# Head tiles of 64 in three transformer blocks: columns by fours, rotation over full rows, halves stacked by DMA

## The chip, the core and the metric

The kernel runs on one core of one Trainium2 chip. The metric is the device time of one execution in microseconds (us); the median of three runs counts.

## The reference

Three different transformer blocks run one after the other over 512 tokens of 1024 channels, in float32. Each has feed-forward parts (2816 wide, gated) and a mixer. The change touches the attention in the mixers of block 1 and of the two layers of block 3. Cut to that:

```python
# block 1: 8 heads of 64, causal, with a forget term
logits = q @ k.T * 64**-0.5 + cum[q] - cum[k]
out = softmax(where(kpos <= qpos, logits, NEG_INF)) @ v
# block 3, two layers: kinds A (8 heads, keys chosen by an index) and B (4 pairs of heads)
q, k = apply_rope(q), apply_rope(k)      # x1*c - x2*s, x2*c + x1*s; x1, x2 the halves of 64
out_a = softmax(where(selected, q @ k.T * scale, -inf)) @ v
out_b = (softmax(q0 @ k0.T) - lam * softmax(q1 @ k1.T)) @ v
```

## The kernel before, in words

Activations lie with channels on the 128 partitions and tokens in the columns. The 512 tokens are two halves of 256 (`hf`), and every phase is written for both halves, the second lagging by some 20 to 30 us (`LAGS`), so that both use a weight while it is in the ring. A product in about float32 accuracy is three fp16 products of high and low halves (`three`, `gemm`): one output tile of 128 x 256 from 1024 channels is 24 matmuls. Weights come in slots of 512 KB on SP's queue into 3 staging buffers (L360), ACT casts the high half (L362), DVE the low half (L363) into a ring of 12.

Nothing fixes the order of the work by hand: a list scheduler orders each engine's instructions at build time by a priority, and a buffer that isn't free holds an instruction back. The priority is a virtual time, advanced with `adv` (2.6 us for one projection), and `boost(us)` moves a group ahead by so many us: rotations have RB = 80, the splitting into heads PB = 10 in block 3 and MB = 80 in block 1.

Keys and queries come out of 8 projection tiles per set: 4 tiles of keys, 4 of queries, each two heads of 64 rows. There are ten such sets: block 1 for each half, and in block 3 two layers, kinds A and B, two halves. In block 3 `rotated` (a function in `mixer3`) takes a tile from PSUM: ACT copies four times 32 rows so that the halves change places (L1286, tile `rsw`), DVE multiplies the tile by the cosine (L1287) and the swapped one by the sine (L1288) and adds them (L1289). It is also used for the three tiles of the index heads (32 wide).

The class `Heads` holds the result. A score is two matmuls over 128 rows: a key tile has its fp16 high half in 64 rows and its low half in the other 64; a query tile has the high half in both places, and a second query tile (`low`) has the low half in 64 rows and zeros, set by a memset on POOL, in the rest. `put` fills them for each head of the tile: ACT writes the high half (L676, in block 1 L679 with the scale), DVE the low half (L677, L680), and for queries ACT copies the high half into the other 64 rows (L682). `scores` issues the two matmuls per 256 keys. PSUM has two buffers per half for projections (`pmm`); a half has 7 temporary buffers of 1 KB per partition (`t1k`).

After a set of heads come the value projections, two `token_gemm` of 24 matmuls with 512 columns, and then attention: scores, row maximum (L641), exponential (L646), reciprocal (L648), transposes and the product with the values. Beside kind B's heads the index scores are computed, and DVE takes the 16 rounds of eight maxima (L1342, L1343).

Of the kernel before, what the change touches and what calls it, by code (L numbers as in the profile page):

```python
# [11 lines left out]
F16 = mybir.dt.float16  # L12
# [7 lines left out]
TH = 256  # L20
# [55 lines left out]

def pack_tm(w):
    return np.ascontiguousarray(w.reshape(4, 2, 128, 512).transpose(0, 2, 1, 3)).reshape(4, 128, 1024)


def small_cols(w):
# [75 lines left out]
def prepare(inp):  # L157
# [12 lines left out]
        a[f"gu1{n}"] = pack_pair(f("ffn_w_gate")[0, n], f("ffn_w_up")[0, n])  # L170
        a[f"dn1{n}"] = pack_cm(f("ffn_w_down")[0, n])
    w = f("w_in")[0]
    a["m1_qk"] = pack_cm(w[:, 1024:2048])
    a["m1_v"] = pack_tm(w[:, 2048:2560])
    a["m1_f"] = small_cols(w[:, 2560:2568])
    a["m1_u"] = pack_cm(w[:, 0:512])
# [34 lines left out]
    for l in range(2):  # L211
        a[f"gu3{l}"] = pack_pair(f("w_gate_3")[l], f("w_up_3")[l])
        a[f"dn3{l}"] = pack_cm(f("w_down_3")[l])
        w = f("w_in_3")[l]
        iq = w[:, 1536:1792].reshape(D, 4, 2, 2, 16).transpose(0, 1, 3, 2, 4).reshape(D, 256)
        ik = w[:, 1792:1824].reshape(D, 2, 16)
        ike = np.zeros((D, 2, 2, 2, 16), w.dtype)
        for e in range(2):
            ike[:, e, :, e, :] = ik
        a[f"m3_i{l}"] = pack_cm(np.concatenate([iq, ike.reshape(D, 128)], 1))  # L220
        a[f"m3_w{l}"] = small_cols(w[:, 1824:1832])
        a[f"m3_a{l}"] = pack_cm(np.concatenate([w[:, 512:1024], w[:, 0:512]], 1))
        a[f"m3_va{l}"] = pack_tm(w[:, 1024:1536])
        a[f"m3_b{l}"] = pack_cm(np.concatenate([w[:, 2344:2856], w[:, 1832:2344]], 1))
        a[f"m3_vb{l}"] = pack_tm(w[:, 2856:3368])
        a[f"m3_o{l}"] = pack_cm(f("w_out_3")[l])
    a["cols"] = np.ascontiguousarray(np.concatenate(cols.parts, 1))
# [5 lines left out]
    a["consts"] = np.ascontiguousarray(np.concatenate(list(c.values()), 1))  # L233
    a["foxsel"] = fox_selector()
    a["headrows"] = head_rows()
    a["rope64"] = rope_rows(32)
    a["rope32"] = rope_rows(16)
    return a, cols.at, at

# [4 lines left out]
def tile_three_blocks(ctx: ExitStack, tc: tile.TileContext, d, col_at, con_at, out, phases=None):  # L244
# [13 lines left out]
    kvp = pool("kvp", 9)  # L258
    prp = pool("prp", 3)
    tin = pool("tin", 2)  # L260
    psm = pool("psm", 2, space=bass.MemoryType.PSUM)
    pss = pool("pss", 2, space=bass.MemoryType.PSUM)

# [394 lines left out]
    class Heads:  # L658
# [1 line left out]


        def __init__(self, alloc, hf, query):
            self.t = [alloc(hf, [128, 2, 2, TH], F16, "hd") for _ in range(2)]
            self.low = [alloc(hf, [128, 4, TH], F16, "hl") for _ in range(2)] if query else None
            if query:
                for e in range(2):
                    G.memset(self.low[e][64 - 64 * e:128 - 64 * e], 0.0)

        def put(self, j, src, scale=None):
            t = self.t[j // 2][:, j % 2]  # L670
            for e in range(2):
                a, b = slice(64 * e, 64 * e + 64), slice(64 - 64 * e, 128 - 64 * e)
                hi = t[a, e]
                lo = t[b, e] if self.low is None else self.low[e][a, j]
                if scale is None:
                    S.activation(hi, src[a], AF.Copy)  # L676
                    V.tensor_tensor(lo, src[a], hi, op=OP.subtract)  # L677
                else:
                    S.activation(hi, src[a], AF.Copy, scale=scale)  # L679
                    V.scalar_tensor_tensor(lo, src[a], scale, hi, op0=OP.mult, op1=OP.subtract)  # L680
                if self.low is not None:
                    S.activation(t[b, e], hi, AF.Copy)  # L682

    def scores(s, q, ks, j, e, c, nk):
        for kh, c0, n in keys(nk):
            k = ks[kh].t[j // 2][:, j % 2, e]
            mm(s[:, c0:c0 + n], q.t[j // 2][:, j % 2, e, c], k[:, :n], start=c0 == 0, stop=False)
            mm(s[:, c0:c0 + n], q.low[e][:, j, c], k[:, :n], start=False, stop=False)

    def keys(nk):  # L690
        return [(0, 0, min(nk, TH))] + ([(1, TH, nk - TH)] if nk > TH else [])
# [16 lines left out]
    def mixer1(hf):  # L708
# [21 lines left out]
            m1["carry"] = 0.0  # L730

        kt, qt_ = Heads(kv2k, hf, False), Heads(m2k, hf, True)
        for j in range(8):
            adv(hf, 2.6)
            p = pmm(hf, [128, TH], name="pp")
            gemm(p, W("m1_qk"), (j + 4) % 8 * KD, KD, px)
            with boost(MB):
                (kt if j < 4 else qt_).put(j % 4, p, 1.0 / WS if j < 4 else 0.125 / WS)
        m1["k", hf] = kt

        adv(hf, 2.6)
# [34 lines left out]
        with boost(BOOST["m1a"]):  # L776
            for qt in range(2):
                nk = (2 * hf + qt + 1) * 128
                yb = m2k(hf, name="yb")
                ybs.append(yb)  # L780
                for h in range(8):
                    j = h // 2
                    s = psmall(hf, [128, 512], name="ps")
                    scores(s, qt_, [m1["k", i] for i in range(hf + 1)], j, h % 2, slice(qt * 128, (qt + 1) * 128), nk)
# [468 lines left out]
    def mixer3(hf, l):  # L1253
# [65 lines left out]
        with later(SELB):  # L1319
            for qt in range(2):  # L1320
# [26 lines left out]
        def logits(qs, ks, j, e, qt, nk, bar):  # L1347
            s = psmall(hf, [128, 512], name="ps")
            scores(s, qs, [m3[ks, i] for i in range(hf + 1)], j, e, slice(qt * 128, (qt + 1) * 128), nk)
# [6 lines left out]
        ybs, yas = [], []  # L1356

        kb, qb = Heads(kv2k, hf, False), Heads(m2k, hf, True)
        for j in range(8):
            dst = t1k(hf, name="rot")  # L1360
            rotated(f"m3_b{l}", j, dst, "rope64", 1.0 / WS if j < 4 else 0.125 / WS)
            with boost(PB):
                (kb if j < 4 else qb).put(j % 4, dst)
        m3["kb", hf] = kb
        vb = []
        for tt in range(2):
# [6 lines left out]
        with boost(BOOST["m3b"]):  # L1373
            for qt in range(2):
                nk = (2 * hf + qt + 1) * 128
                nb = nk // 128

                yb = m2k(hf, name="yb")
                ss = tiny(hf, 4, "dss")
                for h in range(4):  # L1380
                    s = logits(qb, "kb", h, 0, qt, nk, None)
                    p0, r0, s0 = softmax(hf, s, nk)
                    p1, r1, _ = softmax(hf, logits(qb, "kb", h, 1, qt, nk, None), nk)
# [17 lines left out]
        for j in range(8):  # L1401
            dst = t1k(hf, name="rot")
            rotated(f"m3_a{l}", j, dst, "rope64", 1.0 / WS if j < 4 else 0.125 / WS)
            with boost(PB):
                (ka if j < 4 else qa).put(j % 4, dst)
        m3["ka", hf] = ka
        va = []
        for tt in range(2):
# [6 lines left out]
        with boost(BOOST["m3a"]):  # L1415
            for qt in range(2):
# [2 lines left out]

                ya = m2k(hf, name="ya")  # L1420
                for h in range(8):
                    s = logits(qa, "ka", h // 2, h % 2, qt, nk, bars.get(qt))
# [102 lines left out]
```

## Time and profile before

| what | value |
|---|---|
| median of 3 runs | 3486.3 us (3482.32 to 3499.97) |
| the profiled execution | 3491.3 us, its span 3489.5 us |
| PE, DVE, ACT busy | 95%, 62%, 44% of the span |
| mean granted clock of TensorE | 0.98 |
| block 1's mixer, block 3's two mixers, by the trace | about 390 to 620, 2100 to 2450, 2780 to 3100 us |

A row of groups reads: line, engine, operation, tile written <- tiles read, shape, count | busy us in all, mean ns of one | idle time of the engine before them and what ended it. Waits are "who waited <- for what". PE's matmuls are pipelined, so a busy PE isn't PE at its peak.

### The profile page before, as it was taken

Reading aid. Unit: us, or ns where it says so; the run is one execution under the profiler, and the core shown is the slowest. Engines: PE = TensorE matmul, PEld = TensorE weight load, DVE = VectorE, ACT = ScalarE, POOL = GpSimd, SP = SyncE. Lnnn points to the kernel's source line nnn. Section 1 sums busy time; section 2 is a strip of 40 time slices with the busy share of each in tenths; the row PEclk is TensorE's granted clock in tenths of the full one; section 3 lists DMA queues with packets and bytes.
Section 4 is the critical chain, followed back from the end, with each engine's and each line's share of the span. In section 5 each row is a group of like instructions: output and inputs, shape, how many; then the busy total and the mean of one; then the engine's idle time right before and its main releaser. Section 6 shows DMA issues by size and latency. Waiting matters only on the chain.

```text
span 3489.5 us, 71768 instructions
## 1 busy us (share of the span) xinstructions
PE 3315.7 (95%) x30120; PEld 2801.9 (80%) x30120; DVE 2154.7 (62%) x5164; ACT 1542.0 (44%) x3337; POOL 19.1 (1%) x24
## 2 busy tenths in 40 slices
PE   8999999999999999998789999889999998999998
PEld 5888767888888888886578887667888876688887
DVE  8953758744374437677984438896544488855433
ACT  4232465433243324424243336886333278843331
POOL 0000000000000000000000000000000000000000
PEclk9999999999999999987899999999999999999999
DMA  8832313233323222201022222112232321123331
GB/s 309 308 110 91 107 55 131 73 103 101 101 91 103 97 98 97 65 5 34 19 85 98 97 100 97 55 43 67 92 103 97 105 86 53 51 68 109 104 98 48
DMA packets 103283, 327.85 MB, mean 94 GB/s; under 512 B 12328, under 2 KB 17832, under 8 KB 102704
## 3 DMA queue, kind: packets, MB, share of 16 engines
q1 hardware_dynamic: 102960, 323.28, 27.8%
q8 instruction: 235, 3.85, 0.4%
q14 instruction: 88, 0.72, 0.1%
HBM read 321.14 MB, written 2.10 MB: 93 GB/s over the span
## 4 chain that ended last, share of the span: by engine, by line
PE 74%; DVE 12%; ACT 10%; issue 2%; DMA 1%; SPq 0%; ACTq 0%; DVEq 0%
PE pgu L314 37%; PE po L314 19%; PE pp L314 4%; PE ps L314 3%; ACT rsw L1286 3%; DVE wr L363 2%; ACT wr L362 2%; DVE mix L963 1%; PE pt L314 1%; PE pT L314 1%; ACT hd L676 1%; PE pxy L314 1%; ACT prob L646 1%; PE pw L314 1%; PE ps L653 1%
## 5 line engine op out<-in xcount | busy, mean ns | idle before, releaser
L314 PEld LDWEIGHTS <-wr 128*128 128x128 f16 x24000 | 2346.8, 98 | 329.9 <-issue 27.6
L314 PE MATMUL pgu<-hh,wr 128*128 128x256 f16 x12672 | 1401.9, 273 | 8.0 <-DVE fac L525 2.3
L363 DVE SCALAR_TENSOR_TENSOR wr<-st,wr 128x1024 f16<-128x1024 f32 x524 | 640.3, 1223 | 348.4 <-ACT wr L362 339.7
L314 PE MATMUL po<-act,wr 128*128 128x256 f16 x6336 | 700.3, 273 | 0.1
L362 ACT ACTIVATE wr<-st 128x1024 f16<-128x1024 f32 x524 | 551.1, 1053 | 316.2 <-PE pgu L314 127.4
L314 PE MATMUL pp<-hh,wr 128*128 128x256 f16 x3072 | 379.3, 274 | 4.3 <-DVE rot L1287 2.1
L522 ACT ACTIVATE fth<-pgu 128x256 f32<-128x256 f32 x264 | 101.0, 383 | 580.7 <-PE pgu L314 580.5
L523 DVE SCALAR_TENSOR_TENSOR fth<-fth,pgu 128x256 f32<-128x256 f32 x264 | 110.9, 420 | 353.2 <-ACT fth L522 353.1
L314 PE MATMUL po<-mix,wr 128*128 128x256 f16 x1536 | 197.3, 281 | 17.6 <-DVE wr L363 9.8
L443 ACT ACTIVATE act<-fac 128x256 f16<-128x256 f32 x264 | 109.9, 416 | 183.0 <-DVE fac L525 182.7
L314 PE MATMUL pt<-wr,hh 128*128 128x512 f16 x576 | 143.9, 380 | 0.7 <-DVE wr L363 0.6
L444 DVE TENSOR_TENSOR act<-fac,act 128x256 f16<-128x256 f32 x264 | 111.3, 422 | 49.2 <-ACT act L443 48.8
L491 DVE TENSOR_TENSOR acc<-acc,sq 128x256 f32<-128x256 f32 x84 | 35.4, 421 | 149.9 <-ACT sq L490 149.9
L1286 ACT ACTIVATE rsw<-pp 32x256 f32<-32x256 f32 x304 | 114.1, 375 | 19.9 <-PE pp L314 15.6
L525 DVE SCALAR_TENSOR_TENSOR fac<-fth,pgu 128x256 f32<-128x256 f32 x264 | 110.7, 419 | 7.7
L431 ACT ACTIVATE sq<-x 128x256 f32<-128x256 f32 x154 | 56.0, 409 | 134.2 <-DVE x L500 129.6
L484 ACT ACTIVATE y<-po 128x256 f32<-128x256 f32 x64 | 24.4, 382 | 204.6 <-PE po L314 204.6
L963 DVE SCALAR_TENSOR_TENSOR mix<-glu,cols,mix 128x256 f32<-128x256 f32 x240 | 101.9, 475 | 0.1
L314 PEld LDWEIGHTS <-hh 128*128 128x128 f16 x768 | 62.2, 99 | 47.3 <-issue 1.6
L641 DVE TENSOR_REDUCE amx<-ps 128x1 f32<-128x128 f32 (+3 forms) x160 | 77.1, 486 | 34.5 <-PE ps L314 32.9
L500 DVE SCALAR_TENSOR_TENSOR x<-po,x 128x256 f32<-128x256 f32 x64 | 27.0, 422 | 108.9 <-PE po L314 108.8
L646 ACT ACTIVATE prob<-ps,amx 128x128 f32<-128x128 f32 (+3 forms) x160 | 84.0, 525 | 18.9 <-DVE amx L641 17.4
(357 smaller groups left out, 2926.4 us busy)
## 6 DMA issues: line engine op xcount, KB each, us to landing
st<-in_gu_dram SPq DMA_DIRECT2D x264, 512.0 KB, 3.5
st<-in_dn_dram SPq DMA_DIRECT2D x132, 512.0 KB, 3.5
adw<-in_w_ada_dram SPq DMA_DIRECT2D x112, 256.0 KB, 5.5
st<-in_m_o_dram SPq DMA_DIRECT2D x32, 512.0 KB, 3.5
adr<-in_w_ada_dram SPq DMA_DIRECT2D x16, 512.0 KB, 10.2
st<-in_m_b_dram SPq DMA_DIRECT2D x16, 512.0 KB, 4.1
st<-in_m_a_dram SPq DMA_DIRECT2D x16, 512.0 KB, 3.6
st<-in_m_s_dram SPq DMA_DIRECT2D x14, 512.0 KB, 3.8
```

The costliest lines, as they stand in the source:

```text
L314: return PE.matmul(out_, lhsT=l, rhs=r, start=start, stop=stop, skip_group_check=True)
L362: S.activation(r[:, 0], st, AF.Copy, scale=WS)
L363: V.scalar_tensor_tensor(r[:, 1], st, WS, r[:, 0], op0=OP.mult, op1=OP.subtract)
L443: S.activation(hi, src, AF.Copy)
L444: V.tensor_tensor(lo, src, hi, op=OP.subtract)
L522: S.activation(t, p[:, 0], AF.Tanh, scale=0.5 / WS)
L523: V.scalar_tensor_tensor(t, t, 1.0, p[:, 0], op0=OP.add, op1=OP.mult)
L525: V.scalar_tensor_tensor(a, t, 0.5 / WS / WS / AS, p[:, 1], op0=OP.mult, op1=OP.mult)
L641: V.tensor_reduce(nm, s[:, :nk], axis=AX.X, op=OP.max, negate=True)
L646: S.activation(p[:, :nk], s[:, :nk], AF.Exp, bias=nm, scale=scale, accum_out=sm)
L963: V.scalar_tensor_tensor(cc(j), gl[:, i:i + TH], dw[:, j * 31 + i:j * 31 + i + 1], cc(j), op0=OP.mult, op1=OP.add)
L1286: S.activation(sw[a:a + 32], p[c:c + 32], AF.Copy, scale=scale)
```

## The change

Weight columns of keys and queries are laid out by fours on the host: of four heads the first halves (4 x 32 columns) make one tile, the second halves the next. Two projections share a PSUM tile of 128 x 2 x 256, and partner rows of the rotation then lie in the same partition. The sine and cosine tables become 32 rows repeated four times. DVE forms the two sine products, multiplies the pair by the cosine in place in PSUM and adds; one ACT copy makes the high half of the pair, one DVE subtraction the low half. Both halves are stored to a DRAM tile, and loads of 32 rows x 4 heads x 256 columns bring them back in the stacked form: 2 stores and 4 loads for a pair of key tiles, 2 stores and 6 loads for queries, all on SP's queue. A head is now index `h` in a tile of four. The boost of `put` in block 3 becomes RB. The index heads stay as they are.

```diff
+def fours(w):
+    return w.reshape(len(w), -1, 4, 2, 32).transpose(0, 1, 3, 2, 4).reshape(len(w), -1)
...
-    a["m1_qk"] = pack_cm(w[:, 1024:2048])
+    a["m1_qk"] = pack_cm(fours(np.concatenate([w[:, 1536:2048], w[:, 1024:1536]], 1)))
...
-    a["rope64"] = rope_rows(32)
+    a["rope64"] = np.ascontiguousarray(np.stack([np.concatenate([t] * 4, 0) for t in rope(64)], 1))
...
+    away = pool("away", 1, space=bass.MemoryType.DRAM)
...
-            self.t = [alloc(hf, [128, 2, 2, TH], F16, "hd") for _ in range(2)]
+            self.hf = hf
+            self.t = [alloc(hf, [128, 4, TH], F16, "hd") for _ in range(2)]
             self.low = [alloc(hf, [128, 4, TH], F16, "hl") for _ in range(2)] if query else None
-            if query:
-                for e in range(2):
-                    G.memset(self.low[e][64 - 64 * e:128 - 64 * e], 0.0)
+            for t in self.low or ():
+                G.memset(t[64:128], 0.0)
...
+        def put(self, g, p, scale, tab=None):
+            hf = self.hf
+            hi, lo = (t1k(hf, [128, 2, TH], F16, n) for n in ("hi", "lo"))
+            if tab is None:
+                S.activation(hi, p, AF.Copy, scale=scale)
+                V.scalar_tensor_tensor(lo, p, scale, hi, op0=OP.mult, op1=OP.subtract)
+            else:
+                r = [t1k(hf, name="rot") for _ in range(2)]
+                for b in range(2):
+                    V.scalar_tensor_tensor(r[b], p[:, 1 - b], scale if b else -scale, tab[:, 1], op0=OP.mult, op1=OP.mult)
+                V.scalar_tensor_tensor(p, p, scale, tab[:, 0, None, :].to_broadcast([128, 2, TH]), op0=OP.mult, op1=OP.mult)
+                for b in range(2):
+                    V.tensor_tensor(p[:, b], p[:, b], r[b], op=OP.add)
+                S.activation(hi, p, AF.Copy)
+                V.tensor_tensor(lo, p, hi, op=OP.subtract)
+            kept = away.tile([128, 2, 2, TH], F16, name=f"heads{len(aways)}")
+            aways.append(kept)
+            nc.sync.dma_start(out=kept[:, 0], in_=hi)
+            nc.sync.dma_start(out=kept[:, 1], in_=lo)
+            src = lambda z, b: kept[:, z, b].rearrange("(h r) c -> r h c", r=32)
+            for b in range(2):
+                rows = lambda n: slice(64 * n + 32 * b, 64 * n + 32 * b + 32)
+                nc.sync.dma_start(out=self.t[g][rows(0)], in_=src(0, b))
+                if self.low is None:
+                    nc.sync.dma_start(out=self.t[g][rows(1)], in_=src(1, b))
                 else:
...
+                    nc.sync.dma_start(out=self.t[g][rows(1)], in_=src(0, b))
+                    nc.sync.dma_start(out=self.low[g][rows(0)], in_=src(1, b))
...
+    def scores(s, q, ks, h, c, nk):
         for kh, c0, n in keys(nk):
...
+            k = ks[kh].t[h // 4][:, h % 4]
+            mm(s[:, c0:c0 + n], q.t[h // 4][:, h % 4, c], k[:, :n], start=c0 == 0, stop=False)
+            mm(s[:, c0:c0 + n], q.low[h // 4][:, h % 4, c], k[:, :n], start=False, stop=False)
+
+    def by_fours(hf, w, px, heads, scale, us, tab=None):
+        for g in range(2):
+            for n in range(2):
+                p = pmm(hf, [128, 2, TH], name="pp")
+                for b in range(2):
+                    adv(hf, 2.6)
+                    gemm(p[:, b], W(w), (4 * n + 2 * g + b) * KD, KD, px, bank=b == 0)
+                with boost(us):
+                    heads[n].put(g, p, scale * (1.0, 0.125)[n], tab)
...
-        for j in range(8):
-            dst = t1k(hf, name="rot")
-            rotated(f"m3_b{l}", j, dst, "rope64", 1.0 / WS if j < 4 else 0.125 / WS)
-            with boost(PB):
-                (kb if j < 4 else qb).put(j % 4, dst)
+        by_fours(hf, f"m3_b{l}", px, (kb, qb), 1.0 / WS, RB, tabs["rope64"])
```

Kind A and block 1 (with MB and no table) call `by_fours` in the same way, the weights of both kinds are laid out by `fours`, and the callers of `scores` pass the head's number.

## Rows read from the trace of the kernel before

**Rows 1.** The page: busy time by engine, and PE, DVE and ACT in 40 slices.
```profile
PE 3315.7 (95%) x30120; PEld 2801.9 (80%) x30120; DVE 2154.7 (62%) x5164; ACT 1542.0 (44%) x3337; POOL 19.1 (1%) x24
...
PE   8999999999999999998789999889999998999998
...
DVE  8953758744374437677984438896544488855433
ACT  4232465433243324424243336886333278843331
```

**Rows 2.** The page: the chain that ended last, by engine and by line.
```profile
PE 74%; DVE 12%; ACT 10%; issue 2%; DMA 1%; SPq 0%; ACTq 0%; DVEq 0%
PE pgu L314 37%; PE po L314 19%; PE pp L314 4%; PE ps L314 3%; ACT rsw L1286 3%; DVE wr L363 2%; ACT wr L362 2%; DVE mix L963 1%; PE pt L314 1%; PE pT L314 1%; ACT hd L676 1%; PE pxy L314 1%; ACT prob L646 1%; PE pw L314 1%; PE ps L653 1%
```

**Rows 3.** Busy time by stretch: length, then busy us (instructions) of each engine, clock, DMA.
```profile
2150.00:2400.00 250.00, 220.22 (x1737) 164.10 (x1736) 218.57 (x626) 208.16 (x567) 3.35 (x4) 0.99 0.15 49
2850.00:3050.00 200.00, 174.01 (x1372) 127.26 (x1369) 178.75 (x515) 170.05 (x469) 1.89 (x2) 1.00 0.16 52
400.00:550.00 150.00, 144.49 (x1096) 103.45 (x1095) 99.45 (x288) 95.46 (x236) 0.00 (x0) 1.00 0.20 66
2500.00:2600.00 100.00, 100.00 (x918) 89.63 (x917) 48.99 (x79) 36.36 (x60) 0.00 (x0) 1.00 0.32 106
```

**Rows 4.** Groups of DVE in 2100:2450: count, busy us, mean ns, idle before.
```profile
L1287 DVE SCALAR_TENSOR_TENSOR rot<-pp,rope 128x256 f32<-128x256 f32 x38 | 16.0, 422 | 10.3 <-ACT rsw L1286 9.5
L1289 DVE TENSOR_TENSOR rot<-rot,rsw 128x256 f32<-128x256 f32 x38 | 15.8, 416 | 0.2
L1288 DVE TENSOR_TENSOR rsw<-rsw,rope 128x256 f32<-128x256 f32 x38 | 15.8, 415 | 0.0
L677 DVE TENSOR_TENSOR hd<-rot,hd 64x256 f16<-64x256 f32 x32 | 13.4, 420 | 1.0
L677 DVE TENSOR_TENSOR hl<-rot,hd 64x256 f16<-64x256 f32 x32 | 13.3, 415 | 1.9 <-ACT hd L676 1.6
...
L444 DVE TENSOR_TENSOR mix<-pch,mix 128x512 f16<-128x512 f32 x4 | 2.8, 692 | 1.8 <-ACT mix L443 1.6
```

**Rows 5.** Groups of ACT in the same stretch.
```profile
L1286 ACT ACTIVATE rsw<-pp 32x256 f32<-32x256 f32 x152 | 57.0, 375 | 11.1 <-PE pp L314 8.8
...
L676 ACT ACTIVATE hd<-rot 64x256 f16<-64x256 f32 x64 | 26.3, 411 | 3.9 <-DVE rot L1289 2.9
...
L682 ACT ACTIVATE hd<-hd 64x256 f16<-64x256 f16 x32 | 13.3, 414 | 0.7
...
L443 ACT ACTIVATE mix<-pch 128x512 f16<-128x512 f32 x4 | 2.4, 591 | 0.6 <-PE pch L696 0.5
```

**Rows 6.** Groups of the whole span: the first block's head copies, all query copies.
```profile
L682 ACT ACTIVATE hd<-hd 64x256 f16<-64x256 f16 x80 | 33.1, 414 | 1.9
...
L679 ACT ACTIVATE hd<-pp 64x256 f16<-64x256 f32 x32 | 11.9, 377 | 16.2 <-PE pp L314 11.9 <-DVE hd L680 3.0 <-DVE hl L680 0.9
...
L680 DVE SCALAR_TENSOR_TENSOR hl<-pp,hd 64x256 f16<-64x256 f32 x16 | 6.7, 420 | 1.4 <-ACT hd L679 0.9
...
L680 DVE SCALAR_TENSOR_TENSOR hd<-pp,hd 64x256 f16<-64x256 f32 x16 | 6.6, 421 | 2.1 <-ACT hd L679 1.8
```

**Rows 7.** DMA issues of the whole span: count, KB each, median us to landing.
```profile
out_dram<-x SPq DMA_DIRECT2D x16, 128.0 KB, 2.0
...
ident<-in_consts_dram SPq DMA_DIRECT2D x1, 64.0 KB, 2.2
...
masks<-in_consts_dram SPq DMA_DIRECT2D x2, 64.0 KB, 3.9
```

**Rows 8.** Timeline of SP in 3458.5:3463: start, us, eight output stores.
```profile
3458.93 3.80 SPq L1446 DMA_DIRECT2D out_dram<-x  x8
```

**Rows 9.** Timeline of PE in 2268:2275: start, us, one value projection.
```profile
2268.61 5.34 PE L314 MATMUL pt<-wr,hh 128*128 128x512 f16 x24
```

**Rows 10.** Waits of the DMA queue in 2100:2450: us in total, times, longest.
```profile
SPq L360 <- DVE wr L363: 207.6, 27, 39.1
```

**Rows 11.** The groups of DVE in 2100:2450 once more: the softmax reciprocals.
```profile
L648 DVE RECIPROCAL ars<-asm 128x1 f32<-128x1 f32 x64 | 10.0, 159 | 14.1 <-ACT prob L646 13.6
```

More of the change, by code (lines that the diff above doesn't have):

```diff
@@ L221, in prepare @@
         a[f"m3_w{l}"] = small_cols(w[:, 1824:1832])
-        a[f"m3_a{l}"] = pack_cm(np.concatenate([w[:, 512:1024], w[:, 0:512]], 1))
+        a[f"m3_a{l}"] = pack_cm(fours(np.concatenate([w[:, 512:1024], w[:, 0:512]], 1)))
         a[f"m3_va{l}"] = pack_tm(w[:, 1024:1536])
-        a[f"m3_b{l}"] = pack_cm(np.concatenate([w[:, 2344:2856], w[:, 1832:2344]], 1))
+        a[f"m3_b{l}"] = pack_cm(fours(np.concatenate([w[:, 2344:2856], w[:, 1832:2344]], 1)))
         a[f"m3_vb{l}"] = pack_tm(w[:, 2856:3368])
@@ L662, in __init__ @@
         def __init__(self, alloc, hf, query):
-            self.t = [alloc(hf, [128, 2, 2, TH], F16, "hd") for _ in range(2)]
+            self.hf = hf
+            self.t = [alloc(hf, [128, 4, TH], F16, "hd") for _ in range(2)]
             self.low = [alloc(hf, [128, 4, TH], F16, "hl") for _ in range(2)] if query else None
-            if query:
-                for e in range(2):
-                    G.memset(self.low[e][64 - 64 * e:128 - 64 * e], 0.0)
[L669 to L677, printed above, removed]
-                else:
[L679 to L682, printed above, removed]
@@ L684, in scores @@
-    def scores(s, q, ks, j, e, c, nk):
-        for kh, c0, n in keys(nk):
-            k = ks[kh].t[j // 2][:, j % 2, e]
-            mm(s[:, c0:c0 + n], q.t[j // 2][:, j % 2, e, c], k[:, :n], start=c0 == 0, stop=False)
-            mm(s[:, c0:c0 + n], q.low[e][:, j, c], k[:, :n], start=False, stop=False)
+            for t in self.low or ():
[25 more added lines that the diff above has]
+                    nc.sync.dma_start(out=self.t[g][rows(1)], in_=src(1, b))
+                else:
+                    nc.sync.dma_start(out=self.t[g][rows(1)], in_=src(0, b))
+                    nc.sync.dma_start(out=self.low[g][rows(0)], in_=src(1, b))
@@ new lines, in tile_three_blocks @@
+    aways = []
+    def scores(s, q, ks, h, c, nk):
+        for kh, c0, n in keys(nk):
+            k = ks[kh].t[h // 4][:, h % 4]
[10 more added lines that the diff above has]
+                    heads[n].put(g, p, scale * (1.0, 0.125)[n], tab)
@@ L732, in mixer1 @@
         kt, qt_ = Heads(kv2k, hf, False), Heads(m2k, hf, True)
-        for j in range(8):
[L734 to L738, printed above, removed]
+        by_fours(hf, "m1_qk", px, (kt, qt_), 1.0 / WS, MB)
         m1["k", hf] = kt
@@ L781, in mixer1 @@
                 for h in range(8):
-                    j = h // 2
                     s = psmall(hf, [128, 512], name="ps")
-                    scores(s, qt_, [m1["k", i] for i in range(hf + 1)], j, h % 2, slice(qt * 128, (qt + 1) * 128), nk)
+                    scores(s, qt_, [m1["k", i] for i in range(hf + 1)], h, slice(qt * 128, (qt + 1) * 128), nk)
                     mm(s[:, :nk], m1["sel"][0:72, h], m1["cum"][0:72, :nk], start=False, stop=False)
@@ L1346, in mixer3, with logits @@
                 bars[qt] = mb
-        def logits(qs, ks, j, e, qt, nk, bar):
+        def logits(qs, ks, h, qt, nk, bar):
             s = psmall(hf, [128, 512], name="ps")
-            scores(s, qs, [m3[ks, i] for i in range(hf + 1)], j, e, slice(qt * 128, (qt + 1) * 128), nk)
+            scores(s, qs, [m3[ks, i] for i in range(hf + 1)], h, slice(qt * 128, (qt + 1) * 128), nk)
             if bar is None:
@@ L1358, in mixer3 @@
         kb, qb = Heads(kv2k, hf, False), Heads(m2k, hf, True)
-        for j in range(8):
-            dst = t1k(hf, name="rot")
-            rotated(f"m3_b{l}", j, dst, "rope64", 1.0 / WS if j < 4 else 0.125 / WS)
-            with boost(PB):
-                (kb if j < 4 else qb).put(j % 4, dst)
+        by_fours(hf, f"m3_b{l}", px, (kb, qb), 1.0 / WS, RB, tabs["rope64"])
         m3["kb", hf] = kb
@@ L1380, in mixer3 @@
                 for h in range(4):
-                    s = logits(qb, "kb", h, 0, qt, nk, None)
+                    s = logits(qb, "kb", 2 * h, qt, nk, None)
                     p0, r0, s0 = softmax(hf, s, nk)
-                    p1, r1, _ = softmax(hf, logits(qb, "kb", h, 1, qt, nk, None), nk)
+                    p1, r1, _ = softmax(hf, logits(qb, "kb", 2 * h + 1, qt, nk, None), nk)
                     V.scalar_tensor_tensor(r1, r1, m3["nlam", l], s0, op0=OP.mult, op1=OP.mult)
@@ L1400, in mixer3 @@
         ka, qa = Heads(kv2k, hf, False), Heads(m2k, hf, True)
[L1401 to L1405, printed above, removed]
+        by_fours(hf, f"m3_a{l}", px, (ka, qa), 1.0 / WS, RB, tabs["rope64"])
         m3["ka", hf] = ka
@@ L1421, in mixer3 @@
                 for h in range(8):
-                    s = logits(qa, "ka", h // 2, h % 2, qt, nk, bars.get(qt))
+                    s = logits(qa, "ka", h, qt, nk, bars.get(qt))
                     p, rs, _ = softmax(hf, s, nk)
```

## The prediction

> **What bounds the kernel now.** I read the page first, then the busy time by stretch, then the lines of the two busy stretches, then the waits. The page says that PE is busy for 95% of the span [rows 1], so the change can only earn what PE loses. The forty slices say where that is: DVE rises to 8 and 9 tenths and ACT to 6 to 8 around slices 25 to 27 and 33 to 35, the two third-block mixers, which with the first-block mixer are the places that the change touches. A feed-forward stretch shows PE at its pace: 918 matmuls of 256 columns in 100 us with no idle time, 0.109 us each, DVE at half. In 2150 to 2400 us and in 2850 to 3050 us DVE is busy for 218.57 of 250 us (87%) and 178.75 of 200 (89%), ACT for 208.16 (83%) and 170.05 (85%), and PE sits idle for 29.8 and 26.0 us [rows 3]. So there two engines that evacuate and rotate are close to full, and PE waits for them. The chain of waits agrees: 12% of the span lies on DVE and 10% on ACT, and 3% (some 105 us) on the ACT line that swaps the halves for the rotation, 1% on the head copies [rows 2]. In the first-block mixer (400 to 550 us) DVE and ACT are at two thirds and PE idles for 5.5 us only [rows 3].
>
> **What is removed on ACT and DVE.** All counts are for one third-block layer. Of 38 rotations, 6 are those of the index heads, which stay; 32 change. On ACT each has four swaps of 0.375 us, 48.0 us in all; the 64 head copies are 26.3 us and the 32 copies of the query halves 13.3 us [rows 5]. That is 87.6 us. On DVE the 32 rotations take three operations of 0.422, 0.415 and 0.416 us, 40.1 us, and the 64 low halves 26.7 us [rows 4]: 66.8 us.
>
> **What is added on ACT and DVE.** Per pair of tiles, 16 pairs a layer. ACT makes one fp16 copy of 128x512 out of PSUM, as the row of the mixed channels does in 0.591 us [rows 5]: 9.5 us. Net ACT loses 78 us. DVE has two products of 256 columns out of PSUM (2 x 0.422), one product of 512 columns in place in PSUM, two additions of 256 in place (2 x 0.42), and one subtraction of 512 to fp16, for which the 512-column row reads 0.692 us [rows 4]. No row shows DVE writing PSUM in place. From below I price the 512-column product at the 0.692 of that row; from above at two halves of 0.422, so 0.844, and the subtraction the same. I take 0.692, because that row has the same number of columns, also from PSUM. A pair is then 0.844 + 0.692 + 0.84 + 0.692 = 3.07 us, a layer 49.1 us, and net DVE loses 17.7 us; at the upper price a pair is 3.37 us and DVE loses 12.9.
>
> **What of it lies on the path.** DVE is the fuller engine, so I let the stretches shrink with its load at an unchanged fill: 17.7 x 250 / 218.57 = 20.2 us, and 17.7 x 200 / 178.75 = 19.8 us. Together 40 us (29 at the upper price). The 78 us that ACT sheds per layer I count at nothing beyond that: they are covered by DVE, which ends last after ACT is emptied. If they count too, that is rival B.
>
> **First-block mixer.** There is no rotation there. Gone are 32 ACT copies of 0.377 us and 16 of the 80 query copies (0.414 us), and 32 DVE subtractions, 13.3 us [rows 6]; added are 8 ACT copies of 0.591 and 8 DVE operations of 0.692. ACT sheds 14 us, DVE 7.8, but neither is full, and PE idles for 5.5 us [rows 3]. I take half of that idle time, 3 us, between none and all.
>
> **PSUM and PE.** The number of matmuls, their shapes and their contraction over 128 rows are the same, so PE's own work is unchanged. A PSUM buffer now holds two tiles instead of one and is held until the subtraction has read it, 0.59 us of ACT and 3.07 of DVE. The next pair but one needs it, and a pair is 5.24 us of PE (48 matmuls of 0.109), so the hold is hidden behind the other buffer; without that cover it would cost up to 3.7 us per pair. Memsets, buffer counts and weight casts do not change; the low halves' memsets are off the path on POOL.
>
> **The way through DRAM.** Each pair adds two stores of 128 KB and four loads (keys) or six (queries) of 64 KB, all on SP, 28 per set of heads, 112 a layer. SP issues stores of 128 KB back to back in 3.80 us for eight, 0.475 us each [rows 8], so 53 us of SP a layer. A store lands 2.0 us after its issue, a 64 KB load took 2.2 us or 3.9 us [rows 7]. The last query pair therefore needs after its subtraction: 0.475 + 2.0 (store) + 6 x 0.475 (issue of six loads) + 3.9 = 9.2 us, or 7.5 us with the faster load; before, the copy that stood there was 0.41 us. What hides it: the value projections that follow each set of heads, two of 24 matmuls with 5.34 us each [rows 9], 10.7 us of the same half, beside the other half's work. So I cost it at nothing; without cover it is up to 9 us for each of 10 attention starts (2 layers x 2 kinds x 2 halves, and 2 in the first block).
> Queued behind these on SP stand the weight loads. SP already waits 207.6 of 350 us there for a staging buffer to be cast [rows 10], so weights are ahead of need, and a hold-up of some 7 us per pair, which a stage of several buffers absorbs, costs nothing.
> The rows show eight stores going out 0.475 us apart while each takes 2.0 us to land, so transfers on one queue overlap. The Trainium skill ("DMA: Bandwidth & Descriptors", Rules for kernel authors) speaks against cutting a transfer by partitions: transfers to disjoint partition halves share the same engines and serialize, and one transfer over 128 partitions is better. By that rule six loads end to end would be an estimated 6 x 2.2 = 13.2 us instead of 2.9 + 2.2, and the start of each attention would no longer be covered; that is the case of rival C, and the rows of stores speak for overlap.
>
> **The sum.** The profiled execution took 3491.3 us (span 3489.5 and 1.8 around it). 3491.3 - 40 - 3 = 3448. That execution is 5.0 us above the median of 3486.3, so against the median I say 3443 us.
>
> **The rivals.** A is the forecast above: DVE stays the bound of the two stretches, 3443; with the upper price 3454, and 3469 if only two fifths of its gain reach PE.
> B: PE becomes the bound. ACT's swaps stand on the chain for some 105 us, and once 78 us a layer are gone the two engines no longer hand work back and forth. Then all idle time of PE in these stretches could go: 29.8 + 26.0 + 5.5 = 61 us, 3425 against the median. Counting matmuls at 0.109 us (1737 and 1372 of them, 189 and 150 us of work) would leave 111 us, but the value projections are 512 columns wide and take twice that, so not all of it is there; I go down to 3395.
> D: the time is not on the path. DVE also sat 14.1 us idle in the first mixer before the softmax reciprocals, nearly all until ACT's exponentials ended [rows 11]; if chains like softmax and the selection by maxima set the pace, freed engine time turns into idle time, and some 10 us are gained: 3476.
> C, the other side: the heads come late. The place is the first score matmul of a set, the price 9.2 us after the subtraction, the cover 10.7 us of value projections. If the other half's stores and loads, or a weight load that waits for its staging buffer, stand ahead on SP, the delay doubles to 18.4 us and 7.7 us are bare at each of 10 starts: 77 us lost against 43 won, 3491.3 + 34 - 5 = 3520. It decides when more than 4.3 us stay uncovered per start. Against it: most of what SP does there is waiting. For it: SP works in order, and each load waits for its store.
> That the change does not do what it says would be that DVE's work in PSUM costs more than the upper price; it is in A's bounds.
>
> **How the numbers follow.** A 0.40, B 0.25, D 0.20, C 0.15. A measurement of this kernel can tell about 0.5% from no change, 17.4 us here. Faster (under 3469): 0.39 of A, all of B, 0.03 of D: 0.67. The same: 0.17 of D, 0.01 of A and 0.01 of C: 0.19. Slower: 0.14. The range reaches from 3395, which leaves out some 0.04 of B, to 3495, which leaves out most of C: about 0.17 is outside. A's own range is 3430 to 3469.
>
> **What would show it.** Right: the swap rows fall from 152 to 24 a layer, ACT's busy share in the two mixers falls to about half, DVE's rows there sum to 17 us less a layer, and both stretches end some 20 us earlier, with the feed-forward stretches unchanged. In-place products of 512 columns near 0.69 us. Wrong: PE or its weight loads waiting for a DMA into the head tiles (C), weight casts on ACT waiting for their loads (SP held up), DVE's share falling with the stretches as long as before (D), or PE's idle time there near zero (B).

## The result, and the profile after

The changed kernel took 3430.73 us (median of four runs, 3425.46 to 3438.27), the kernel before 3484.31: ratio 0.9849, 95% interval 0.9829 to 0.9868, some 53 us. The forecast was 3443 us, within 3395 to 3495.

From the page of the changed kernel, the lines that answer to [rows 1] and [rows 2]: busy time, PE, DVE and ACT in 40 slices, the chain by engine and by line.

```profile
PE 3295.0 (96%) x30113; PEld 2794.9 (82%) x30120; DVE 2105.7 (61%) x5012; ACT 1372.9 (40%) x2881; POOL 18.7 (1%) x24
...
PE   8999999999999999998879999999999999999998
...
DVE  8952758844374436598894436996544379845443
ACT  4232356433243324434243334565433255553331
...
PE 77%; DVE 15%; ACT 4%; issue 2%; DMA 2%; ACTq 0%; SPq 0%; DVEq 0%
PE pgu L320 38%; PE po L320 20%; PE pp L320 5%; PE ps L320 4%; DVE wr L369 2%; PE pt L320 2%; DVE mix L989 2%; PE ps L659 1%; ACT wr L368 1%; PE pT L320 1%; PE pxy L320 1%; PE pgl L320 1%; DVE acc L438 1%; PE pw L320 1%; DVE nh L480 1%
```

ACT's busy time fell by 169 us (1542.0 to 1372.9), DVE's by 49, and neither swaps nor head copies are left among the first lines of the chain, where ACT went from 10% to 4%. PE and DVE each have 3 points more of the chain.

Where in the span the time went is read from marks that both kernels have: the last matmul of the gate and up part (tile pgu) of a feed-forward, which is the end of "first to last start" in its row. First the kernel before, then the changed one; the five rows of each are the feed-forwards after block 1's mixer, before block 2's mixer, after it, after the first and after the second mixer of block 3.

```profile
L314 PE MATMUL pgu<-hh,wr x2112: 269/273/421, 636.6 to 897.3; 128*128 128x256 f16 x192
...
L314 PE MATMUL pgu<-hh,wr x1390: 272/273/273, 1079.8 to 1253.5; 128*128 128x256 f16 x199
...
L314 PE MATMUL pgu<-hh,wr x1057: 272/273/273, 1899.8 to 2036.7; 128*128 128x256 f16 x177
...
L314 PE MATMUL pgu<-hh,wr x1782: 270/273/273, 2499.8 to 2715.9; 128*128 128x256 f16 x198
...
L314 PE MATMUL pgu<-hh,wr x1822: 269/273/273, 3159.7 to 3373.3; 128*128 128x256 f16 x183
```

```profile
L320 PE MATMUL pgu<-hh,wr x2112: 269/273/421, 631.7 to 892.3; 128*128 128x256 f16 x192
...
L320 PE MATMUL pgu<-hh,wr x1362: 272/273/273, 1079.8 to 1250.4; 128*128 128x256 f16 x195
...
L320 PE MATMUL pgu<-hh,wr x944: 272/273/273, 1899.8 to 2024.3; 128*128 128x256 f16 x189
...
L320 PE MATMUL pgu<-hh,wr x1410: 272/273/273, 2499.7 to 2675.2; 128*128 128x256 f16 x177
...
L320 PE MATMUL pgu<-hh,wr x1247: 272/273/273, 3159.8 to 3310.2; 128*128 128x256 f16 x179
```

The changed kernel is ahead by 5.0 us, 3.1, 12.4, 40.7 and 63.1. So block 1's mixer gave 5 us by these marks, block 3's two 28.3 and 22.4, 50.7 together. The 5 us are within the scatter of that first mark, which in the other profiles of this study lies from 4 us behind to 7 us ahead. The 9.3 us in block 2 are not the change's: nothing is touched there, and in the other profiles block 2 is 2 to 16 us shorter than in that one profile of the kernel before, also in those of kernels that leave block 1 or block 3 as it was. What differs there is the granted clock: from 1253 to 2037 us it was 0.93 in that profile, 0.94 in the changed kernel's and 0.95 in that of `act_back` below. That profile's own time was also 7 us above the median (3491.3 against 3484.3).

The two full stretches and that of block 1, which answer to [rows 3]; columns as there:

```profile
2150.00:2400.00 250.00, 240.34 (x1914) 181.89 (x1916) 210.02 (x587) 148.34 (x399) 1.89 (x2) 0.99 0.30 94
2850.00:3050.00 200.00, 192.94 (x1528) 148.44 (x1530) 159.90 (x427) 119.75 (x322) 0.95 (x1) 1.00 0.29 91
400.00:550.00 150.00, 145.57 (x1116) 105.69 (x1114) 94.28 (x270) 82.57 (x202) 0.00 (x0) 1.00 0.34 105
```

PE's idle time fell from 29.8 to 9.7 us and from 26.0 to 7.1 us (the windows stand still while the changed kernel is ahead, so they don't hold quite the same work). DVE is at 84% and 80%, after 87% and 89%; ACT is down to 59% and 60%, after 83% and 85%. In block 1 PE idles for 4.4 us instead of 5.5.

The groups that stand in the place of [rows 4] and [rows 5], in 2100 to 2450 us (DVE, then ACT):

```profile
L687 DVE TENSOR_TENSOR pp<-pp,rot 128x256 f32<-128x256 f32 x32 | 13.5, 422 | 0.1
...
L684 DVE SCALAR_TENSOR_TENSOR rot<-pp,rope 128x256 f32<-128x256 f32 x32 | 12.1, 416 | 2.5 <-PE pp L320 2.3
...
L685 DVE SCALAR_TENSOR_TENSOR pp<-pp,rope 128x512 f32<-128x512 f32 x16 | 11.0, 689 | 0.0
L689 DVE TENSOR_TENSOR lo<-pp,hi 128x512 f16<-128x512 f32 x16 | 11.0, 685 | 0.1
...
L654 DVE RECIPROCAL ars<-asm 128x1 f32<-128x1 f32 x64 | 10.0, 157 | 14.3 <-ACT prob L652 14.0
```

```profile
L688 ACT ACTIVATE hi<-pp 128x512 f16<-128x512 f32 x16 | 9.5, 594 | 6.9 <-DVE pp L687 6.9
...
L1312 ACT ACTIVATE rsw<-pp 32x256 f32<-32x256 f32 x24 | 9.0, 375 | 3.4 <-PE pp L320 3.1
```

Per layer these are 16 pairs: DVE has 49 us in place of 66.8, ACT 9.5 in place of 87.6, and the swaps that are left (24) belong to the index heads. The last of the DVE rows is the one of [rows 11]; it is unchanged.

The way through DRAM: DMA issues of the whole span (count, KB, us to landing), and SP's timeline (start, us) with the loads of two query pairs, which go out among each other.

```profile
hd<-heads SPq DMA_DIRECT2D x160, 64.0 KB, 2.0
...
heads<-hi SPq DMA_DIRECT2D x40, 128.0 KB, 1.7
heads<-lo SPq DMA_DIRECT2D x40, 128.0 KB, 1.7
...
hl<-heads SPq DMA_DIRECT2D x40, 64.0 KB, 2.0
```

```profile
2163.44 0.34 SPq L692 DMA_DIRECT2D heads<-hi  x1
2164.16 0.34 SPq L693 DMA_DIRECT2D heads<-lo  x1
2164.55 0.43 SPq L702 DMA_DIRECT2D hl<-heads  x1
...
2169.79 0.43 SPq L702 DMA_DIRECT2D hl<-heads  x1
2170.32 22.33 SPq L366 DMA_DIRECT2D st<-in_m_a_dram  x4
```

Stores land in 1.7 us, loads in 2.0. SP sends a load every 0.48 us (12 of them start from 2164.55 to 2169.79), and the weight loads follow behind them.

### The profile page after: what moved, and what is told of

The parts are those of the page before. It is cut to its first block, busy times and chain, and to the rows that moved or that the text cites. A ratio compares the mean times of both kernels' runs of the same rounds, so it can differ in the third digit from the quotient of the medians.

```text
span 3426.1 us, 71629 instructions
## 1 busy us (share of the span) xinstructions
PE 3295.0 (96%) x30113; PEld 2794.9 (82%) x30120; DVE 2105.7 (61%) x5012; ACT 1372.9 (40%) x2881; POOL 18.7 (1%) x24
## 4 chain that ended last, share of the span: by engine, by line
PE 77%; DVE 15%; ACT 4%; issue 2%; DMA 2%; ACTq 0%; SPq 0%; DVEq 0%
PE pgu L320 38%; PE po L320 20%; PE pp L320 5%; PE ps L320 4%; DVE wr L369 2%; PE pt L320 2%; DVE mix L989 2%; PE ps L659 1%; ACT wr L368 1%; PE pT L320 1%; PE pxy L320 1%; PE pgl L320 1%; DVE acc L438 1%; PE pw L320 1%; DVE nh L480 1%
## 5 line engine op out<-in xcount | busy, mean ns | idle before, releaser
L497 DVE TENSOR_TENSOR acc<-acc,sq 128x256 f32<-128x256 f32 x84 | 35.3, 420 | 150.2 <-ACT sq L496 150.2
L438 DVE TENSOR_TENSOR acc<-acc,sq 128x256 f32<-128x256 f32 x166 | 69.7, 420 | 21.6 <-ACT sq L437 19.2
```

Of the source, the lines that this page charges most:

```text
L438: V.tensor_tensor(acc, acc, t, op=OP.add)
```

## The experiments

Times are compared as ratios to the kernel before, timed on the same chip in the same rounds. The changed kernel's own is 0.9849. Microseconds beside a ratio are differences of medians; the kernel before had 3482 to 3485 us in all rounds.

**Each block alone.** In `m1_only` block 3 keeps the old heads, in `m3_only` block 1 does (below; OldHeads is the class of the kernel before).

```diff
-        kt, qt_ = Heads(kv2k, hf, False), Heads(m2k, hf, True)
-        by_fours(hf, "m1_qk", px, (kt, qt_), 1.0 / WS, MB)
+        kt, qt_ = OldHeads(kv2k, hf, False), OldHeads(m2k, hf, True)
+        for j in range(8):
+            adv(hf, 2.6)
+            p = pmm(hf, [128, TH], name="pp")
+            gemm(p, W("m1_qk"), (j + 4) % 8 * KD, KD, px)
+            with boost(MB):
+                (kt if j < 4 else qt_).put(j % 4, p, 1.0 / WS if j < 4 else 0.125 / WS)
```

> Only block 1 takes the new heads; block 3 is as before. By the theory that the gain comes from the two full stretches of block 3's mixers, about 5 us are gained (the marks of the changed kernel's trace show 4.6 us by the end of block 1's mixer): ratio to before near 0.9985. The 9 us that the changed kernel gained in block 2, which the change does not touch, either come along (then 14 us, 0.996: they follow from how block 1 left the schedule) or not.

> Only block 3 takes the new heads. Expected 51 us of the 54 to 63 gained (28 in its first layer, 22 in its second, by the marks of the changed kernel's trace): ratio near 0.985. If the gains of the two blocks were tied together, less: 0.99 or more.

Measured: 0.9993 (0.9974 to 1.0013) and 0.9879 (0.9851 to 0.9906). The gain is block 3's; block 1's can't be told from nothing. In time, `m3_only` lies between its two bounds, and its 44 us and the 1 us of `m1_only` fall short of the 53 of the whole. By the marks of its profile block 3 gave 51.5 us, as expected. Part of the gap is the granted clock: the four runs of `m3_only` had a mean of 0.980, those of the changed kernel 0.982, and among the 13 runs of the kernel before in those rounds the fastest (3470 us) had 0.987, the slowest (3501 us) 0.977. So a comparison of few runs is good to some 10 us, and small differences below are read from the marks too.

**The loads put back.** ACT's load and DVE's, each alone and both, into the changed kernel:

```diff
+                for _ in range(8):
+                    S.activation(hi[0:32, 0], ones[0:32], AF.Copy)
+                for _ in range(4 if self.low is None else 8):
+                    S.activation(hi[0:64, 0], ones[0:64], AF.Copy)
                 S.activation(hi, p, AF.Copy)
...
+                V.tensor_tensor(lo[:, 0], ones, ones, op=OP.mult)
+                V.tensor_tensor(lo[:, 1], ones, ones, op=OP.mult)
+                V.tensor_tensor(lo[:, 0, 0:128], ones1, ones1, op=OP.mult)
                 V.tensor_tensor(lo, p, hi, op=OP.subtract)
```

> The changed kernel, with as much ACT work put back in each pair of block 3 as was taken away (8 copies of 32x256 and 4 or 8 of 64x256, 87.6 us a layer, of a constant into the high-half tile, which is then overwritten). Theory DVE (DVE's load sets the length of the two stretches, ACT's relief is covered): no more than 10 us of the gain are lost, ratio to before up to 0.988. Rival ACT (the swaps on ACT set the length): most of the 51 us of block 3 are lost, ratio 0.997 or more.

> The changed kernel, with 1.12 us of DVE work put back in each pair of block 3 (two products of 256 columns and one of 128 of a constant into the low-half tile, which is then overwritten), 17.9 us a layer, as much as DVE was relieved of. Theory DVE: some 40 us are lost, 20 a layer, ratio to before near 0.996. Rival ACT: less than 10 us are lost, ratio up to 0.988.

Measured: `act_back` 0.9909 (0.9877 to 0.9942), 3449.0 us; `dve_back` 0.9839 (0.9809 to 0.9869), 3426.2 us. DVE's load costs nothing; ACT's costs some 18 us (21 by the ratios), over a third of the gain. Neither theory holds as it stood, and that of DVE falls outright. The loads were smaller than meant, as the pages of `act_back` and `dve_back` show (the changed kernel has DVE 2105.7, ACT 1372.9):

```profile
PE 3297.4 (96%) x30120; PEld 2792.8 (81%) x30120; DVE 2108.3 (61%) x5012; ACT 1510.7 (44%) x3329; POOL 18.7 (1%) x24
```

```profile
PE 3290.7 (96%) x30120; PEld 2791.8 (82%) x30120; DVE 2126.6 (62%) x5108; ACT 1371.9 (40%) x2881; POOL 18.7 (1%) x24
```

ACT's busy time rose by 138 us and DVE's by 21, over both layers. The new heads of block 3 alone (`m3_only`) had taken 156 from ACT and 40 from DVE. The copies and products put back depend on nothing before them, and the records of such neighbours overlap: two products of 0.42 us on DVE start 0.34 us apart in the trace of `dve_back`. So `dve_back` returns half of DVE's relief. At the fill of 87% that should still have cost some 24 us by the theory of DVE, an estimate; nothing was lost. The two stretches, first of `act_back`, then of `dve_back`:

```profile
2150.00:2400.00 250.00, 238.89 (x1883) 179.62 (x1882) 208.04 (x571) 207.44 (x597) 1.89 (x2) 0.98 0.31 94
2850.00:3050.00 200.00, 187.98 (x1477) 143.31 (x1476) 156.59 (x423) 161.50 (x474) 0.95 (x1) 0.99 0.31 95
```

```profile
2150.00:2400.00 250.00, 242.04 (x1930) 185.14 (x1928) 218.52 (x626) 149.40 (x405) 1.89 (x2) 0.99 0.30 93
2850.00:3050.00 200.00, 195.22 (x1545) 150.23 (x1544) 167.19 (x457) 120.79 (x322) 0.95 (x1) 1.00 0.28 89
```

With 87% and 84% of DVE busy in the second (87% and 89% before the change), PE idles for only 8.0 and 4.8 us. A fill of 87% was not what held PE.

**Load taken out of the kernel before.** The other way round; first `before_less_act`, then `before_less_dve`:

```diff
-                for b in range(4):
+                for b in range(0 if tab == "rope64" else 4):
...
-                V.tensor_tensor(sw, sw, tabs[tab][:, 1], op=OP.mult)
+                V.tensor_tensor(sw, ones if tab == "rope64" else sw, tabs[tab][:, 1], op=OP.mult)
```

```diff
-                V.tensor_tensor(sw, sw, tabs[tab][:, 1], op=OP.mult)
+                if tab != "rope64":
+                    V.tensor_tensor(sw, sw, tabs[tab][:, 1], op=OP.mult)
```

> The kernel before without the four ACT swaps of each rotation in block 3's heads of 64; the sine product reads a constant tile instead, so the rotation is left out of the result and DVE's operations stay as many. 48 us of ACT a layer are gone. If ACT's load and its place at the head of each rotation held PE up, most of block 3's 51 us are gained: ratio to before 0.988 or less. If ACT's share is what its load cost when it was put back (17 us of marks), 0.995.

> The kernel before without the sine product on DVE in block 3's heads of 64 (the rotation is left out of the result), 13.3 us of DVE a layer; ACT's swaps stay. Theory DVE of the prediction: 13.3 x 250/218.57 and 13.3 x 200/178.75, some 30 us gained, ratio 0.991. If DVE's load doesn't bind, as the load put back says: within 7 us, ratio 0.998 to 1.002.

Measured: 0.9914 (0.9887 to 0.9942) without the swaps, 30 us; 1.0024 (1.0008 to 1.0040) without the sine product. Taking operations of 13.3 us a layer from the engine that was 87% full (its busy time fell by 8 a layer) made nothing faster. What less ACT work does is best seen in one row of the groups of the whole span, the score matmuls (the first of each two; busy, mean ns | idle time of PE before them, and what ended it). Before, changed, before without swaps, before without the sine product:

```profile
L314 PE MATMUL ps<-hd 128*128 128x256 f16 (+1 forms) x240 | 56.6, 254 | 24.8 <-ACT prob L646 13.2 <-ACT ps L1392 7.0 <-ACT hd L682 1.2
```

```profile
L320 PE MATMUL ps<-hd 128*128 128x256 f16 (+1 forms) x240 | 56.0, 253 | 3.6 <-ACT prob L652 2.1 <-ACT rl L1359 0.2 <-ACT ya L1447 0.2
```

```profile
L314 PE MATMUL ps<-hd 128*128 128x256 f16 (+1 forms) x240 | 57.3, 255 | 14.1 <-ACT prob L646 5.9 <-ACT ps L1392 2.7 <-DVE hl L677 1.2
```

```profile
L314 PE MATMUL ps<-hd 128*128 128x256 f16 (+1 forms) x240 | 57.2, 255 | 30.3 <-ACT prob L646 14.4 <-ACT ps L1393 9.2 <-ACT rl L1334 2.7
```

PE stood 24.8 us before its score matmuls, mostly until ACT had finished an exponential (prob) or a square (ps), the last user of a PSUM tile that the next score needs (a half has two of them). After the change 3.6 us are left; without the swaps alone 14.1; with less DVE work 30.3. The product with the values waits in the same way, for ACT's copy of the transposed probabilities (probt); before, then changed:

```profile
L314 PE MATMUL ps<-vb,probt 128*128 128x128 f32 x160 | 27.2, 295 | 12.5 <-ACT probt L655 12.2
```

```profile
L320 PE MATMUL ps<-vb,probt 128*128 128x128 f32 x160 | 27.6, 295 | 3.0 <-ACT probt L661 2.6
```

The timeline of the kernel before shows one such wait. The transposes end at 2259.69 us, ACT does four swaps first, then the copy, and PE has sat idle for 0.67 us when the product begins:

```profile
2259.25 0.44 PE L653 MATMUL ps<-ident,prob 128*128 128x128 f32 x2 [0.52 <-DVE prob L1385]
...
2259.45 1.54 ACT L1286 ACTIVATE rsw<-pp 32x256 f32<-32x256 f32 x4
...
2261.01 0.38 ACT L655 ACTIVATE probt<-ps 128x256 f32<-128x256 f32 x1
...
2261.45 0.71 PE L314 MATMUL ps<-vb,probt 128*128 128x128 f32 x4 [0.67 <-ACT probt L655]
```

So ACT's queue, in which swaps and head copies stood ahead of the softmax's steps, kept PE waiting. With the index scores, whose wait fell from 7.1 to 0.9 us, these groups make up 37 of the 43 us by which PE's idle time in the whole span fell (span less PE's busy time on the two pages). The copies put back in `act_back` don't bring these waits back, though:

```profile
L320 PE MATMUL ps<-hd 128*128 128x256 f16 (+1 forms) x240 | 56.6, 254 | 6.0 <-ACT prob L652 2.4 <-ACT rl L1363 1.5 <-ACT ps L1418 1.0
```

PE's idle time is 11 us longer there than in the changed kernel, spread over many groups.

**Two other parts of the change alone, in the kernel before.** In `before_pairs` two tiles of block 3 share a PSUM tile (turned is the old rotation, from PSUM on; the heads of kind a are changed likewise); in `before_pb80` only the priority differs.

```diff
-        for j in range(8):
-            dst = t1k(hf, name="rot")
-            rotated(f"m3_b{l}", j, dst, "rope64", 1.0 / WS if j < 4 else 0.125 / WS)
...
+        for j0 in range(0, 8, 2):
+            p2 = pmm(hf, [128, 2, TH], name="pp")
+            for j in (j0, j0 + 1):
+                adv(hf, 2.6)
+                gemm(p2[:, j - j0], W(f"m3_b{l}"), j * KD, KD, px, bank=j == j0)
+            for j in (j0, j0 + 1):
+                dst = t1k(hf, name="rot")
+                turned(p2[:, j - j0], dst, "rope64", 1.0 / WS if j < 4 else 0.125 / WS)
...
```

```diff
-PB = 10
+PB = 80
```

> The kernel before with one part of the change alone: in block 3 two projection tiles share a PSUM tile, so four tiles of a half can wait in PSUM and not two; swaps, rotation and head copies as before. If the depth of PSUM is what let PE run ahead, some 20 to 34 us are gained (ratio 0.990 to 0.994); if it is ACT's or DVE's work, nothing (0.998 to 1.002).

> The kernel before with the priority of the splitting into heads in block 3 raised from 10 to 80 us, as the change has it. If the order was what mattered, up to 20 us gained (0.994); otherwise no difference beyond 7 us (0.998 to 1.002).

Measured: 1.0041 (1.0022 to 1.0060) and 1.0002 (0.9986 to 1.0019). Neither the depth of PSUM nor the priority gives anything alone; the pairs cost a little with the old chain, perhaps since a tile is held until the rotation of both is through, which was not tried by itself.

**What is left beside the loads.**

> The changed kernel with both loads put back in block 3, the 87.6 us a layer of ACT and the 17.9 us of DVE, beside the chain as in the two runs before; the result is unchanged. If the two loads bind together (each engine has room alone, not both), most of the gain goes: ratio to before 0.996 or more. If what remains of the gain comes from the shorter chain of hand-overs for each tile, the time stays where ACT's load alone put it: ratio 0.989 to 0.993.

Measured: 0.9913 (0.9885 to 0.9941), 3456.5 us. With both engines about as full as before the change (DVE 88%, ACT 82% in the first stretch, as the rows show), still 26 us are gained, half of the whole.

```profile
2150.00:2400.00 250.00, 233.91 (x1860) 177.46 (x1858) 218.84 (x627) 204.39 (x590) 1.89 (x2) 0.98 0.29 94
2850.00:3050.00 200.00, 188.65 (x1487) 143.74 (x1487) 173.38 (x493) 162.93 (x485) 0.95 (x1) 0.99 0.29 92
```

The copies put back hang on nothing, so the scheduler may place them where ACT is free; the swaps had to come between PE and DVE. That was tried next, in the place of the swaps:

```diff
                 for b in range(2):
+                    for a in range(0, 128, 32):
+                        S.activation(r[b][a:a + 32], p[a:a + 32, 1 - b], AF.Copy)
                     V.scalar_tensor_tensor(r[b], p[:, 1 - b], scale if b else -scale, tab[:, 1], op0=OP.mult, op1=OP.mult)
```

> The changed kernel with eight ACT copies of 32x256 a pair ahead of the sine products, written into the products' tiles and overwritten by DVE, so that each pair again begins on ACT and DVE waits for it: 48 us of ACT a layer, in the place that the swaps had, with the PSUM tile held for as long. If the place on the chain counts beyond the load: 20 us or more lost, ratio 0.991 or more. If only ACT's load counts, 48 of 87.6 us cost about 10 of the 20 us that the full load cost: 0.986 to 0.989.

Measured: 0.9880 (0.9852 to 0.9907), 3443.2 us, 12 us lost. By the bounds set, the load counts and the place does not count beyond it. But its four runs had the highest mean granted clock of the study, 0.985, and the interval overlaps that of the changed kernel. The marks say otherwise. The third mark lies before block 3, the fifth behind its second mixer; what each kernel gained between the two against the kernel before, one profile each:

| kernel | gain in block 3, us |
|---|---|
| changed, `m3_only`, `extra_hop` | 50.7, 51.5, 51.3 |
| `dve_back` | 55.3 |
| `act_back` | 33.6 |
| `act_first` | 29.5 |
| `both_back` | 22.1 |
| `before_less_act` | 24.0 |
| `before_less_dve`, `before_pairs` | -8.4, -14.3 |
| `before_pb80`, `m1_only` | -2.6, -0.5 |

Kernels that should agree lie within some 3 us. By these marks `act_first` loses 21 us with 48 us of copies a layer, `act_back` 17 with nearly twice the copies. In proportion to the copies 9 of the 21 would be load and 12 the place, an estimate; so the place counts too. The score matmuls wait again:

```profile
L320 PE MATMUL ps<-hd 128*128 128x256 f16 (+1 forms) x240 | 56.2, 254 | 15.6 <-ACT prob L652 5.9 <-ACT rl L1361 4.5 <-ACT ps L1416 4.1
```

**The way through DRAM made longer.**

```diff
+            again = away.tile([128, 2, 2, TH], F16, name=f"again{len(aways)}")
+            for z in range(2):
+                nc.sync.dma_start(out=again[:, z], in_=kept[:, z])
-            src = lambda z, b: kept[:, z, b].rearrange("(h r) c -> r h c", r=32)
+            src = lambda z, b: again[:, z, b].rearrange("(h r) c -> r h c", r=32)
```

> The changed kernel with a second trip through DRAM: each half of each pair is copied from its DRAM tile to another before it is loaded, two more DMAs on SP and some 2 to 3 us more until the heads are there, for all ten sets. If the way through DRAM is covered, as the prediction has it: no difference beyond 7 us, ratio to before 0.983 to 0.987. Rival C (the heads come late): 10 starts with 2 to 3 us each, 20 to 30 us lost, 0.991 or more.

Measured: 0.9845 (0.9817 to 0.9874), 3432.4 us: no difference. The extra copies took 2.6 us each (issues of that kernel), PE's wait before the scores stays at 4.0 us, and none of it is for a DMA (PE's one such wait in that trace, 9.6 us, is for the tile adr):

```profile
again<-heads SPq DMA_DIRECT2D x80, 128.0 KB, 2.6
hd<-again SPq DMA_DIRECT2D x160, 64.0 KB, 2.1
```

```profile
L320 PE MATMUL ps<-hd 128*128 128x256 f16 (+1 forms) x240 | 56.1, 253 | 4.0 <-ACT prob L652 2.6 <-ACT rl L1362 0.2
```

**More work moved from ACT to DVE.**

```diff
-                    S.activation(yb[:, h * 128:(h + 1) * 128], o_, AF.Copy, scale=r0)
+                    V.tensor_scalar(yb[:, h * 128:(h + 1) * 128], o_, r0, None, op0=OP.mult)
...
-                    S.activation(ya[:, h * 64:h * 64 + 64], o_, AF.Copy, scale=rs)
+                    V.tensor_scalar(ya[:, h * 64:h * 64 + 64], o_, rs, None, op0=OP.mult)
```

> The changed kernel with the evacuation of the attention's results in block 3 (the tiles ya and yb, scaled by a column) moved from ACT to DVE, 15.7 us of ACT a layer. If less ACT work still lets PE run on: 3 to 8 us gained, ratio to before 0.982 to 0.984. If PE's own work is the bound now, nothing: 0.984 to 0.987.

Measured: 0.9832 (0.9800 to 0.9864), 3429.1 us. It can't be told from the changed kernel (0.9849). With PE idle for 17 of the 450 us of the two stretches there is little left for a lighter ACT to give.

## Why the prediction was right, and where it wasn't

**The size and the sign: right**, 43 us forecast (3486 to 3443), 53 measured; block 3 was to give 40 and gave 51 by the marks, block 1 was to give 3 and gave 5 by the marks, which is within their scatter and within the noise of `m1_only`. That the size came out so near is partly luck, since its largest term had the wrong cause.

**The prices: right.** The in-place product of 512 columns took 0.689 us (0.692 forecast, 0.844 as the upper end), the subtraction 0.685, ACT's copy 0.594 (0.591). A pair on DVE was forecast at 3.07 us; the rows give 2 x 0.416 + 0.689 + 2 x 0.422 + 0.685 = 3.05.

**The step that failed** is "DVE is the fuller engine, so I let the stretches shrink with its load at an unchanged fill", and with it "the 78 us that ACT sheds per layer I count at nothing". Both were wrong, and they offset each other: DVE's relief alone is worth nothing (half of it put back 0.9839, load taken out of the kernel before 1.0024), ACT's is worth 18 us (load put back beside the chain) to 30 us (swaps taken out of the kernel before, load and place together). Rival B was nearer: PE's idle time in the stretches fell from 55.8 to 16.7 us, as ACT's swaps left the chain, and its 3425 us is nearer to the 3431 measured than the forecast is. But ACT's load put back brings only 6 of these 39 us back, so the load alone is not the whole of it. The rows spoke for ACT: the chain had 3% on the swaps and 1% on the head copies, while DVE's rotation was not among its lines there [rows 2]. I set the busier engine above the engine that the chain named. The Trainium skill ("Trainium Kernel Development and Optimization", Best Practices) has occupancy as fine for judging how near engines other than PE are to their limit. How near an engine is to its own limit did not say here which one held PE up: DVE at 87% and ACT at 83% looked alike, and only ACT's work cost time, since its queue stood between PE and its next PSUM tile.

**Rival C, the heads too late: excluded.** The 10.7 us of cover were enough; even 2.6 us more per pair cost nothing. The parts of its price were lower than I took: 1.7 us for a store, 2.0 for a load; only the issue, 0.48 us each, was as forecast. The rule of the Trainium skill ("DMA: Bandwidth & Descriptors", Rules for kernel authors) that transfers to disjoint partition halves serialize did not bite here: loads issued 0.48 us apart land in 2.0 us each, so their times from issue to landing overlap, and SP's issue sets their pace. Whether their bytes move one after the other, no row shows. **Rival D** is excluded by the result.

**Open.** `act_back` puts 18 of the 53 us down to ACT's load, `before_less_act` 30 to the swaps' load and place together; `both_back` leaves 26 us (22 by the marks) that no load explains. By elimination they are not the depth of PSUM alone nor the priority alone. The swaps' place is part of them, some 12 us by the estimate from the marks. For the rest there remains what follows the rotation: for a key tile four, for a query tile six operations on 64 rows that hand over between ACT and DVE (two high halves, two low halves, for queries two copies) against one ACT copy and one DVE subtraction for two tiles, or parts that only work together. That was not tried by itself. Open too is whether DVE's load counts once ACT's is there: the times of `act_back` and `both_back` can't be told apart, but their marks differ by 11 us.

## What to carry to other kernels

An engine's busy share says how much it works, not that it holds anything up: add the same load again or take it away before reckoning with it. Where several pieces of work share ACT, ask whose instructions stand ahead of the one that frees PE's next PSUM tile; short copies that only move rows between partitions are the first to go. Moving rows by DMA through DRAM cost nothing here, where other matmuls stand between the store and the first use. When load is put back to test a cause, read from the page how much busy time it really added, and put it also in the place that the old work had.

## What had not been expected of the hardware

DVE working in place in PSUM, which no row of the kernel before showed, costs no more than reading it: 0.689 us for 512 columns in place, 0.685 us from PSUM to a fp16 tile. And with DVE 87% busy over 250 us PE was idle for only 8 of them (`dve_back`). Two products on DVE that don't depend on each other take 0.42 us each but start 0.34 us apart, so busy time is less than the sum of the rows.
